# Combining two expert outputs per token: twelve-token tiles in four buffers, and sixteen-token tiles in three with per-token arithmetic

## The chip, the cores and the metric

The kernel runs on one core of a Trainium2 chip. A core has several engines with instruction streams of their own; here VectorE (DVE), ScalarE (ACT) and SyncE (SP) matter. VectorE and ScalarE compute on the core's on-chip memory, which has 128 partitions. Transfers between the chip's large memory (HBM) and the on-chip memory are issued by SyncE or ScalarE and carried out by 16 DMA engines. The metric is the device time of one execution in microseconds (us), the median of several runs. The span, which the profile uses, runs from the first to the last instruction of one profiled execution.

## The reference

```python
batch, seq, hidden, n_experts, k = 16, 1024, 512, 8, 2
# expert_outputs: (batch, seq, k, hidden) float32; combine_weights: (batch, seq, k) float32

def reference(expert_outputs, combine_weights):
    weights = combine_weights[..., np.newaxis]
    return np.sum(expert_outputs * weights, axis=2).astype(np.float32)
```

Each of the 16 x 1024 = 16384 tokens has two vectors of 512 numbers and two weights. The output is the weighted sum of the two vectors. A token is 4 KB of input and 2 KB of output; in all 67 MB are read and 34 MB written. With 128 partitions, each partition handles 128 tokens.

## The kernel before

The tokens of a partition are cut into ten tiles of 12 and a last one of 8. Each tile is loaded, combined in place and stored from the same buffer: the results fill the first half of the tile's bytes. Four buffers rotate, so the load of a tile waits until the store of the tile four places earlier has landed.

The layout: `main` tokens per partition lie in one part of the arrays, and the last tile in a second part, so that each partition reads one contiguous run per tile.

```python
    J, LAST = 12, 8
    main = per - LAST            # per is 128
    eo = expert_outputs.rearrange("b s k h -> (b s) (k h)")
    ...
    def rows(x):
        a = x[0 : P * main, :].rearrange("(p t) f -> p t f", p=P)
        b = x[P * main : n, :].rearrange("(p t) f -> p t f", p=P)
        return lambda t, c: a[:, t : t + c, :] if t < main else b[:, t - main : t - main + c, :]
    ...
    last = main // J
    wpool = ctx.enter_context(tc.tile_pool(name="w", bufs=1))
    ipool = ctx.enter_context(tc.tile_pool(name="in", bufs=4))
    wt = wpool.tile([P, per * k], dt)            # all weights, loaded once through ScalarE's queue
    ...
```

The loop over tiles. Loads go through SyncE's queue. The first load is split in 2 and 10 tokens.

```python
    for g in range(last + 1):
        et = ipool.tile([P, J, k * h], dt)
        ot = et.rearrange("p j f -> p (j f)")[:, 0 : J * h].rearrange("p (j f) -> p j f", f=h)
        t0, c = g * J, J if g < last else LAST

        for a, m in ((0, 2), (2, c - 2)) if g == 0 else ((0, c),):
            nc.sync.dma_start(
                out=et[:, a : a + m],
                in_=eo(t0 + a, m),
                max_dma_last_dim=k * h * 4 if g + a == 0 else None,
            )
```

The first nine tiles are combined by two large VectorE instructions, a product of the whole tile with the weights (line 78) and a sum of its two halves (line 79). Their stores go through ScalarE's queue (line 80).

```python
        if g < last - 1:
            wb = wt[:, g * J * k : (g + 1) * J * k].unsqueeze(2).to_broadcast([P, J * k, h])
            ek = et.rearrange("p j (k h) -> p (j k) h", k=k)
            nc.vector.tensor_tensor(out=ek, in0=ek, in1=wb, op=mult)
            nc.vector.tensor_tensor(out=ot, in0=et[:, :, 0:h], in1=et[:, :, h : 2 * h], op=add)
            nc.scalar.dma_start(out=o(t0, c), in_=ot)
            continue
```

The tenth tile has its first products on ScalarE, a token at a time (line 86), and the second product and the sum as two VectorE instructions (lines 101 and 102). The last tile takes, per token, one ScalarE product and one VectorE multiply-add (line 90). The stores of these two go through SyncE's queue (line 103).

```python
        for i in range(c):
            t = t0 + i
            nc.scalar.activation(
                out=et[:, i, 0:h], in_=et[:, i, 0:h], func=copy, scale=wt[:, 2 * t : 2 * t + 1]
            )
            if g == last:
                nc.vector.scalar_tensor_tensor(
                    out=ot[:, i, :], in0=et[:, i, h : 2 * h],
                    scalar=wt[:, 2 * t + 1 : 2 * t + 2],
                    in1=et[:, i, 0:h], op0=mult, op1=add,
                )
        if g < last:
            ...                                   # w1, x1: second weights, second halves
            nc.vector.tensor_tensor(out=x1, in0=x1, in1=w1.to_broadcast([P, c, h]), op=mult)
            nc.vector.tensor_tensor(out=ot, in0=et[:, :, 0:h], in1=x1, op=add)
        nc.sync.dma_start(out=o(t0, c), in_=ot[:, 0:c])
```

Of the kernel before, what the change touches and what calls it, by code (L numbers as in the profile page):

```python
# [1 line left out]

# [4 lines left out]


@with_exitstack
def kernel(  # L10
    ctx: ExitStack,
    tc: tile.TileContext,
    expert_outputs: bass.AP,
    combine_weights: bass.AP,
    out: bass.AP,
):

    nc = tc.nc  # L20
    b, s, k, h = expert_outputs.shape
    assert k == 2
    n = b * s
    P = nc.NUM_PARTITIONS
    per = n // P
    assert per * P == n
    J, LAST = 12, 8
    main = per - LAST
    assert main % J == 0
    eo = expert_outputs.rearrange("b s k h -> (b s) (k h)")  # L30
    cw = combine_weights.rearrange("b s k -> (b s) k")
    o = out.rearrange("b s h -> (b s) h")
# [7 lines that stand above are left out]
    eo, cw, o = rows(eo), rows(cw), rows(o)  # L40

    dt = mybir.dt.float32
    mult = mybir.AluOpType.mult
    add = mybir.AluOpType.add
    copy = mybir.ActivationFunctionType.Copy

    last = main // J

    wpool = ctx.enter_context(tc.tile_pool(name="w", bufs=1))
    ipool = ctx.enter_context(tc.tile_pool(name="in", bufs=4))  # L50

    wt = wpool.tile([P, per * k], dt)

    for t, c in ((0, main), (main, LAST)):
        nc.scalar.dma_start(
            out=wt[:, k * t : k * (t + c)].rearrange("p (t k) -> p t k", k=k), in_=cw(t, c)
        )

    warm = wpool.tile([P, 1], dt)
    nc.scalar.activation(out=warm, in_=nc.const_aps.tensor(1.0, (P, 1), dt), func=copy)  # L60

    for g in range(last + 1):
        et = ipool.tile([P, J, k * h], dt)

        ot = et.rearrange("p j f -> p (j f)")[:, 0 : J * h].rearrange("p (j f) -> p j f", f=h)
        t0, c = g * J, J if g < last else LAST

        for a, m in ((0, 2), (2, c - 2)) if g == 0 else ((0, c),):
            nc.sync.dma_start(  # L69
                out=et[:, a : a + m],  # L70
                in_=eo(t0 + a, m),
                max_dma_last_dim=k * h * 4 if g + a == 0 else None,
            )
        if g < last - 1:

            wb = wt[:, g * J * k : (g + 1) * J * k].unsqueeze(2).to_broadcast([P, J * k, h])
            ek = et.rearrange("p j (k h) -> p (j k) h", k=k)
            nc.vector.tensor_tensor(out=ek, in0=ek, in1=wb, op=mult)  # L78
            nc.vector.tensor_tensor(out=ot, in0=et[:, :, 0:h], in1=et[:, :, h : 2 * h], op=add)  # L79
            nc.scalar.dma_start(out=o(t0, c), in_=ot)  # L80
            continue


        for i in range(c):
            t = t0 + i
            nc.scalar.activation(  # L86
                out=et[:, i, 0:h], in_=et[:, i, 0:h], func=copy, scale=wt[:, 2 * t : 2 * t + 1]
            )
            if g == last:
                nc.vector.scalar_tensor_tensor(  # L90
                    out=ot[:, i, :],
                    in0=et[:, i, h : 2 * h],
                    scalar=wt[:, 2 * t + 1 : 2 * t + 2],
                    in1=et[:, i, 0:h],
                    op0=mult,
                    op1=add,
                )
        if g < last:
            w1 = wt.rearrange("p (t k) -> p t k", k=k)[:, t0 : t0 + c, 1:2]
            x1 = et[:, :, h : 2 * h]  # L100
            nc.vector.tensor_tensor(out=x1, in0=x1, in1=w1.to_broadcast([P, c, h]), op=mult)  # L101
            nc.vector.tensor_tensor(out=ot, in0=et[:, :, 0:h], in1=x1, op=add)  # L102
        nc.sync.dma_start(out=o(t0, c), in_=ot[:, 0:c])


# [1 line left out]
_INS = ['expert_outputs', 'combine_weights']  # L107
_OUTS = [((16, 1024, 512), 'float32')]


# [23 lines left out]
```

## Time and profile before

| What | Value |
|---|---|
| time, median of 3 runs | 239.17 us (238.93 to 240.34) |
| span of the profiled execution | 237.3 us |
| VectorE busy | 193.9 us |
| ScalarE busy | 14.0 us |
| HBM read and written | 67.24 MB and 33.55 MB, 425 GB/s over the span |
| load of a 12-token tile | 6144 KB, nine times, median 29.9 us from issue to landing |
| store of a 12-token tile | 3072 KB, nine times through ScalarE's queue, median 32.7 us from issue to landing |

Busy time of an engine is the sum of its instructions' durations; two engines can be busy at once. The time from issue to landing of a transfer includes what it spends behind others in its queue. A packet is the piece of a transfer that a DMA engine moves in one go. The chain of waits follows the work that ended last back to the start, at each step to what released it. In a line of instruction groups, L78 means line 78 of the kernel, and `et<-in_expert_outputs_dram` a load into a tile, `out_dram<-et` a store.

### The profile page before, as it was taken

How to read it: one execution, taken by the hardware profiler on the slowest of the kernel's cores; microseconds unless marked ns; L12 is line 12 of the kernel's file. 1: busy time of each engine (PE TensorE's matmuls, PEld its weight loads, DVE VectorE, ACT ScalarE, POOL GpSimd, SP SyncE). 2: the span in 40 equal slices, each digit the busy share in tenths (PEclk: the TensorE clock that was granted, in tenths of full speed). 3: DMA queues.
4: the chain of work that ended last, by engine and by line, in shares of the span. 5: the costliest groups of instructions: out<-in, count | busy, mean ns of one | idle time of the engine just before them, and what ended most of it. 6: DMA issues, size and time to landing. Idle time of an engine off the chain costs nothing.

```text
span 237.3 us, 154 instructions
## 1 busy us (share of the span) xinstructions
DVE 193.9 (82%) x28; ACT 14.0 (6%) x22; POOL 0.2 (0%) x4
## 2 busy tenths in 40 slices
DVE  0008999999999999999999879969996998785710
ACT  2000000000000000000000000000000000740800
POOL 0000000000000000000000000000000000000000
DMA  8999999989899999999897999999997979999997
GB/s 308 443 456 406 398 431 497 398 356 505 356 439 435 427 464 464 398 398 522 348 522 344 452 427 435 464 464 398 398 522 340 530 336 460 458 403 442 402 438 309
DMA packets 3728, 100.80 MB, mean 425 GB/s; under 512 B 528, under 2 KB 656, under 8 KB 912
## 3 DMA queue, kind: packets, MB, share of 16 engines
q1 hardware_dynamic: 2144, 72.35, 71.1%
q10 hardware_dynamic: 1584, 28.44, 27.9%
HBM read 67.24 MB, written 33.55 MB: 425 GB/s over the span
## 4 chain that ended last, share of the span: by engine, by line
DMA 59%; DVE 33%; ACT 2%; DVEq 0%; ACTq 0%; issue 0%; SPq 0%
DMA et<-in_expert_outputs_dram 30%; DMA out_dram<-et 29%; DVE et L78 22%; DVE et L79 11%; ACT et L86 2%; DVE et L90 1%; DVEq L129 0%; ACTq L129 0%; SPq L69 0%; DVEq L78 0%; ACTq L86 0%
## 5 line engine op out<-in xcount | busy, mean ns | idle before, releaser
L78 DVE TENSOR_TENSOR et<-et,wt 128x12288 f32<-128x12288 f32 x9 | 116.6, 12955 | 25.2 <-DMA et<-in_expert_outputs_dram 25.2
L79 DVE TENSOR_TENSOR et<-et 128x6144 f32<-128x6144 f32 x9 | 59.0, 6558 | 0.3
L86 ACT ACTIVATE et<-et,wt 128x512 f32<-128x512 f32 x20 | 12.5, 707 | 209.2 <-DMA et<-in_expert_outputs_dram 209.2
L90 DVE SCALAR_TENSOR_TENSOR et<-et,wt 128x512 f32<-128x512 f32 x8 | 5.6, 748 | 3.9 <-ACT et L86 3.7
L101 DVE TENSOR_TENSOR et<-et,wt 128x6144 f32<-128x6144 f32 x1 | 6.6, 6559 | 2.3 <-DMA et<-in_expert_outputs_dram 2.3
L102 DVE TENSOR_TENSOR et<-et 128x6144 f32<-128x6144 f32 x1 | 6.6, 6559 | 0.9 <-ACT et L86 0.9
L60 ACT ACT_TABLE_LOAD x1 | 1.3, 1283 | 1.7 <-issue 1.7
L60 ACT ACTIVATE warm<-const-float32-1.0 128x1 f32<-128x1 f32 x1 | 0.2, 202 | 0.0
L118 POOL MEMSET const-bfloat16-1.0<- 128x1 bf16 x1 | 0.1, 102 | 0.0
L118 POOL MEMSET const-uint8-127<- 128x1 uint8 x1 | 0.1, 102 | 0.0
L118 POOL MEMSET const-float32-0.0<- 128x1 f32 x1 | 0.1, 99 | 0.2 <-issue 0.2
L118 POOL MEMSET const-float32-1.0<- 128x1 f32 x1 | 0.1, 99 | 0.0
## 6 DMA issues: line engine op xcount, KB each, us to landing
et<-in_expert_outputs_dram SPq DMA_DIRECT2D x9, 6144.0 KB, 29.9
out_dram<-et ACTq DMA_DIRECT2D x9, 3072.0 KB, 32.7
et<-in_expert_outputs_dram SPq DMA_DIRECT2D x1, 5120.0 KB, 17.3
et<-in_expert_outputs_dram SPq DMA_DIRECT2D x1, 4096.0 KB, 25.1
out_dram<-et SPq DMA_DIRECT2D x1, 3072.0 KB, 14.6
out_dram<-et SPq DMA_DIRECT2D x1, 2048.0 KB, 10.0
et<-in_expert_outputs_dram SPq DMA_DIRECT2D x1, 1024.0 KB, 5.4
wt<-in_combine_weights_dram ACTq DMA_DIRECT2D x1, 120.0 KB, 4.4
```

The costliest lines, as they stand in the source:

```text
L60: nc.scalar.activation(out=warm, in_=nc.const_aps.tensor(1.0, (P, 1), dt), func=copy)
L78: nc.vector.tensor_tensor(out=ek, in0=ek, in1=wb, op=mult)
L79: nc.vector.tensor_tensor(out=ot, in0=et[:, :, 0:h], in1=et[:, :, h : 2 * h], op=add)
L86: nc.scalar.activation(out=et[:, i, 0:h], in_=et[:, i, 0:h], func=copy, scale=wt[:, 2 * t : 2 * t + 1])
L90: nc.vector.scalar_tensor_tensor(out=ot[:, i, :], in0=et[:, i, h : 2 * h], scalar=wt[:, 2 * t + 1 : 2 * t + 2], in1=et[:, i, 0:h], op0=mul ...
L101: nc.vector.tensor_tensor(out=x1, in0=x1, in1=w1.to_broadcast([P, c, h]), op=mult)
L102: nc.vector.tensor_tensor(out=ot, in0=et[:, :, 0:h], in1=x1, op=add)
L118: nc = _bacc.Bacc("TRN2", target_bir_lowering=False, num_devices=1)
```

## The change

The tiles become 16 tokens: seven of them, and a last one of the same size, in three buffers in place of four. A row of a load, one partition's part of a tile, is 64 KB, and a row of a store 32 KB. The large VectorE instructions go: in every tile each token takes one ScalarE product and one VectorE multiply-add. The first load is split in 2 and 14 tokens; the last tile is loaded, combined and stored in parts of 12 and 4. The stores go through ScalarE's queue, those of the last tile through SyncE's. It is meant to take work off VectorE, to share it with ScalarE, and to move the same bytes in fewer and longer transfers.

```diff
-    J, LAST = 12, 8
-    main = per - LAST
+    J = 16
+    main = per - J
 ...
-    ipool = ctx.enter_context(tc.tile_pool(name="in", bufs=4))
+    ipool = ctx.enter_context(tc.tile_pool(name="in", bufs=3))
 ...
-    for t, c in ((0, main), (main, LAST)):
+    for t, c in ((0, main), (main, J)):
 ...
-        t0, c = g * J, J if g < last else LAST
+        t0 = g * J
-        for a, m in ((0, 2), (2, c - 2)) if g == 0 else ((0, c),):
+        for a, m in {0: ((0, 2), (2, 14)), last: ((0, 12), (12, 4))}.get(g, ((0, J),)):
             nc.sync.dma_start(
 ...
-        if g < last - 1:
-            ...   # the two large VectorE instructions and their store, as above
-            continue
-        for i in range(c):
-            t = t0 + i
-            nc.scalar.activation(...)
-            if g == last:
+        for a, m in ((0, 12), (12, 4)) if g == last else ((0, J),):
+            for i in range(a, a + m):
+                t = t0 + i
+                nc.scalar.activation(
+                    out=et[:, i, 0:h], in_=et[:, i, 0:h], func=copy, scale=wt[:, 2 * t : 2 * t + 1]
+                )
                 nc.vector.scalar_tensor_tensor(
                     out=ot[:, i, :],
 ...
-        if g < last:
-            ...   # second product and sum of the tenth tile
-        nc.sync.dma_start(out=o(t0, c), in_=ot[:, 0:c])
+            store = nc.scalar if g < last else nc.sync
+            store.dma_start(out=o(t0 + a, m), in_=ot[:, a : a + m])
```

More of the change, by code (lines that the diff above doesn't have):

```diff
@@ L73 @@
             )
-        if g < last - 1:
[L76 to L80, printed above, removed]
-            continue
-        for i in range(c):
-            t = t0 + i
-            nc.scalar.activation(
-                out=et[:, i, 0:h], in_=et[:, i, 0:h], func=copy, scale=wt[:, 2 * t : 2 * t + 1]
-            )
-            if g == last:
+        for a, m in ((0, 12), (12, 4)) if g == last else ((0, J),):
[4 more added lines that the diff above has]
+                )
                 nc.vector.scalar_tensor_tensor(
@@ L97 @@
                 )
-        if g < last:
[L99 to L102, printed above, removed]
-        nc.sync.dma_start(out=o(t0, c), in_=ot[:, 0:c])
+            store = nc.scalar if g < last else nc.sync
+            store.dma_start(out=o(t0 + a, m), in_=ot[:, a : a + m])
 _INS = ['expert_outputs', 'combine_weights']
```

## The prediction

> **What bounds the kernel now.** I read four views, in this order. First the page: the busy shares, the slices and the queues.
>
> ```profile
> DVE 193.9 (82%) x28; ACT 14.0 (6%) x22; POOL 0.2 (0%) x4
> DMA  8999999989899999999897999999997979999997
> DMA packets 3728, 100.80 MB, mean 425 GB/s; under 512 B 528, under 2 KB 656, under 8 KB 912
> q1 hardware_dynamic: 2144, 72.35, 71.1%
> q10 hardware_dynamic: 1584, 28.44, 27.9%
> ```
>
> VectorE is busy 82% of the span, but the two DMA queues (q1 is SyncE's, q10 ScalarE's) together fill 71.1 + 27.9 = 99.0% of the time of the 16 DMA engines. Two limits cannot both hold; the one at 99% does, if it holds in every stage. So second, the chain of waits:
>
> ```profile
> DMA 59%; DVE 33%; ACT 2%; DVEq 0%; ACTq 0%; issue 0%; SPq 0%
> ```
>
> A third of the chain is VectorE. In order of time those are three tiles from 18.6 to 77.1 us and one from 137.7 to 157.2 us: four tiles of 19.5 us, 78 us. To see whether VectorE really holds the kernel there, third, the busy time by stage (length, then DVE, ACT, POOL, clock, DMA share, GB/s):
>
> ```profile
> 18.60:38.00 19.40, 19.33 (x2) 0.00 (x0) 0.00 (x0) 1.00 1.03 446
> 78.00:108.00 30.00, 29.97 (x3) 0.00 (x0) 0.00 (x0) 1.00 1.00 434
> 138.00:168.00 30.00, 27.75 (x3) 0.00 (x0) 0.00 (x0) 1.00 1.01 436
> 220.00:226.50 6.50, 5.57 (x8) 4.94 (x8) 0.00 (x0) 1.00 1.03 442
> 231.50:235.00 3.50, 0.00 (x0) 0.00 (x0) 0.00 (x0) 1.00 1.04 445
> ```
>
> In all of them the DMA engines are full (a share over 1 is a packet counted in the stretch where it starts). The chain takes one releaser at each step, and a tile that computes while older tiles move is on it by name only. Fourth, the timeline of SyncE shows the beat of the loads:
>
> ```profile
> 85.86 0.33 SPq L69 DMA_DIRECT2D et<-in_expert_outputs_dram  x1
> 107.68 0.33 SPq L69 DMA_DIRECT2D et<-in_expert_outputs_dram  x1
> 129.40 0.33 SPq L69 DMA_DIRECT2D et<-in_expert_outputs_dram  x1
> ```
>
> A tile each 21.8 us, where VectorE needs 19.5. The packet records explain 21.8. Each DMA engine carries 8 of the 128 rows of a transfer, one packet a row. Median packet times: 48 KB 1815 ns, 40 KB 1514, 32 KB 1213, 24 KB 912, 16 KB 611; the 4 KB packets of the first load average 201. So a row costs 9 ns + 37.6 ns per KB, whether load or store (16, 24 and 32 KB fall on one line with the rest). Eight load rows and eight store rows are 8 x (1.815 + 0.912) = 21.8 us: the beat of the loads. The kernel moves rows back to back from about 1.8 us to 236 us.
>
> [...] 21.8 us is one load row and one store row in turn, so loads get two thirds of the bytes while both queues have work. [...] the row times here give 1024 B / 37.6 ns = 27.2 GB/s per engine, 435 for 16. [...] The rows stand 480 KB apart before and 448 KB after; no run so far shows 448. [...]
>
> **The change part by part.**
>
> *Arithmetic.* It removes nine pairs of VectorE products and sums (12.95 + 6.56 us for 12 tokens, 1.63 us a token) and the mixed tile before the last. Every token now takes what the last eight took:
>
> ```profile
> L86 ACT ACTIVATE et<-et,wt x20: 704/706/722, 203.0 to 224.2; 128x512 f32<-128x512 f32 x20
> L90 DVE SCALAR_TENSOR_TENSOR et<-et,wt x8: 746/746/753, 220.7 to 225.7; 128x512 f32<-128x512 f32 x8
> ```
>
> The eight ScalarE products took 5.01 us in all, 0.63 a token; the eight multiply-adds 5.78 us, 0.72 a token, the first of them 0.84 us after the load landed (219.85 to 220.69). The two overlap, so a 16-token tile takes 0.84 + 16 x 0.72 = 12.4 us from landing to store, against 19.5 for 12 tokens. VectorE falls to 128 x 0.75 = 95 us busy, ScalarE rises to 128 x 0.71 + 1.5 = 92 us. Neither is near the span. On the end they are worth nothing as long as the queues stay full.
>
> *Transfers.* The bytes are the same. I add up one DMA engine's rows, times 8.
> Before: first load 2 x 0.201 + 1.514; nine loads of 48 KB 16.335; last load 1.213; ten stores of 24 KB 9.120; last store 0.611; weights 0.055. Sum 29.25, times 8 = 234.0 us.
> After: 2 x 0.201 + 2.116 (56 KB); six loads of 64 KB, by the line 9 + 64 x 37.6 = 2417 ns (an estimate, as are 56 KB and 8 KB), 14.50; 1.815 + 0.611; seven stores of 32 KB 8.49; 0.912 + 0.310; weights 0.055. Sum 29.21, times 8 = 233.7 us.
> The difference is the 9 ns of some rows saved: 0.3 us.
>
> *Buffers.* 3 x 16 = 48 tokens, as 4 x 12 was. Does a queue run dry? The first rows move about 1 us after issue (none before 1.6 us), and I allow 1 us from last row to landing. The second part of load 0 lands near 23.5; its 14 tokens are done at 23.5 + 0.84 + 14 x 0.72 = 34.4. Store 0 then shares with load 1 and load 2, 2.417 + 1.213 = 3.63 us a pair, 29.0 us for eight pairs, so it lands near 64.6 and releases load 3. Load 2, with less of its rows moved, lands near 74.3: SyncE's queue still has some 9 us of work when load 3 comes in. Tile 2 is done at 74.3 + 12.4 = 86.7, and store 1 lands near 93.7: ScalarE's queue still has some 5 us after issue time. From there each beat repeats at 29.0 us, with the same margins. ScalarE now issues the stores behind its own arithmetic and waits there for VectorE; it has 29 us for 12.4 of work, so that wait costs nothing.
>
> *End.* Load 7 is released by store 4, near 181. Its 12-token part lands near 214.7, computed at 214.7 + 0.84 + 12 x 0.72 = 224.2. The 4-token part leaves SyncE's queue near 226, store 6 leaves ScalarE's near 224. So the 12-token store, with a microsecond of issue, comes in at 225.3, just in time. It and the 4-token store then take 8 x (0.912 + 0.310) = 9.8 us: near 236, landed near 237. Before, the end was as tight: last store 10.0 us from issue to landing. I count 0 here, with a risk of 0.5 to 1 us.
>
> Sum: 237.3 - 0.3 = 237.0 us of span; the time stands 1.9 above the span (239.17 against 237.3): 238.9 us.
>
> **The rivals.**
>
> *VectorE was the bound.* For it: 82% busy and 78 us of the chain. If those 78 us of tiles (48 tokens at 1.63) shrank to 0.72 a token, 43 us would go, and the time would be 196 us. Against it: rows need 233.7 us at a rate that no size exceeds. Even without any start or end the gain could be at most 237.3 - 233.7 = 3.6 us, 1.5%. I give this nearly nothing.
>
> *Three large buffers starve a queue.* Each new load waits for a whole 4 MB store, and the unit is a third larger. If the margins of 9 and 5 us were misjudged, 1 to 3 us per beat would be lost in four or five beats: 243 to 252 us. Against it: the ratio of bytes and the 48 tokens are unchanged, the queues are served row by row, and compute is 7 us shorter per tile.
>
> *The 64 KB row.* It lies beyond the sizes measured (48 KB at most). If it moved as two packets, loads and stores would share evenly; stores would land sooner and loads later, with full queues all the same; the steps above with even turns end 0.4 us later: 239.3 us. If long rows or the 448 KB distance cost 5% of the load rate, 8 x 19.4 x 0.05 = 7.8 us would come on top: 246.6 us. The straight line from 16 to 48 KB speaks against it.
>
> *The end comes apart.* If the 12-token store misses its moment, the engines idle for what it is late: at 0.8 us a token 1 us, so 239.9 us.
>
> **Range and chances.** The middle is 238.9. A quieter end or fewer long rows (48 KB rows averaged 1823 ns, not 1815, some 0.6 us over the kernel) take it to 237.7; a late last store and the scatter of the times before (238.93 to 240.34) take it to 240.6. Faster by over 2% means under 234.4, a span of 232.5, less than the rows need: 0.02. Slower by over 2%, above 244.0, needs starved queues or slow rows: 0.06. Within 2%: 0.92.
>
> **What would show it.** Right: the queues' shares again sum to about 99%, packets of 64 KB take about 2417 ns, loads are issued 29.0 us apart, VectorE is busy near 95 us with waits on loads, and the slices of the DMA show no hole but the first. Wrong: load issues more than 30 us apart or a lower DMA share in the middle (starved buffers); packets of 64 KB above 2.5 us (the row); a gap in the DMA between 222 and 228 us (the end); or a span under 234 us, which would break the rule that rows cost what their bytes cost.

## The result, and the profile after

| | time, median | span of the profiled execution |
|---|---|---|
| before | 239.52 us (238.93 to 240.34) | 237.3 us |
| changed | 241.18 us (240.93 to 241.78) | 239.8 us |

The ratio of changed to before is 1.0082, with a 95% interval of 1.0061 to 1.0103. The change makes the kernel 0.8% slower. The prediction had 238.9 us and a range up to 240.6. Executions of the kernel before fall in two groups, 73 of 107 near 239.0 us and 34 near 240.3, at the same clock and for a reason that no run here shows; the ratios average over both, while the trace and the span of before are of the first.

The changed kernel's page, busy shares, slices and queues:

```profile
DVE 87.0 (36%) x128; ACT 81.0 (34%) x130; POOL 0.2 (0%) x4
DMA  9999999999999999999999999999999999999895
DMA packets 3155, 100.82 MB, mean 420 GB/s; under 512 B 464, under 2 KB 592, under 8 KB 848
q1 hardware_dynamic: 1856, 71.30, 69.4%
q10 hardware_dynamic: 1296, 29.49, 28.7%
q14 instruction: 3, 0.02, 0.0%
```

VectorE's work has more than halved, as meant, and the DMA engines are full in every slice up to the last three. What is new is the last line: a third queue, named instruction, with three packets. The page of the kernel before has no such line. Those packets are 8 KB each and take 0.309 us; together they are 0.02 of 100.82 MB. (In both traces such packets also lie before the span begins.)

The chain of waits and the beat of the loads in the changed kernel:

```profile
DMA 85%; DVE 6%; ACT 4%; issue 1%; SPq 1%; DVEq 0%; ACTq 0%
```

```profile
67.29 0.33 SPq L68 DMA_DIRECT2D et<-in_expert_outputs_dram  x1
96.25 0.33 SPq L68 DMA_DIRECT2D et<-in_expert_outputs_dram  x1
125.78 0.33 SPq L68 DMA_DIRECT2D et<-in_expert_outputs_dram  x1
154.79 0.33 SPq L68 DMA_DIRECT2D et<-in_expert_outputs_dram  x1
```

The loads are 28.96, 29.53 and 29.01 us apart. Rows cost what they should: 64 KB packets have a median of 2418 ns. So the middle runs at the rate of the rows, and the loss is at the end. Busy time by stage there (length, DVE, ACT, POOL, clock, DMA share, GB/s), changed kernel:

```profile
226.00:228.00 2.00, 0.49 (x1) 0.00 (x0) 0.00 (x0) 1.00 0.62 254
236.00:237.00 1.00, 0.00 (x0) 0.00 (x0) 0.00 (x0) 1.00 1.04 434
237.00:238.00 1.00, 0.00 (x0) 0.00 (x0) 0.00 (x0) 1.00 0.12 49
238.00:239.00 1.00, 0.00 (x0) 0.00 (x0) 0.00 (x0) 1.00 0.02 8
```

The same stretches of the kernel before:

```profile
226.00:228.00 2.00, 0.46 (x1) 0.00 (x0) 0.00 (x0) 1.00 0.92 393
236.00:237.00 1.00, 0.00 (x0) 0.00 (x0) 0.00 (x0) 1.00 0.00 0
```

Two things differ. Between 226 and 228 us the DMA engines are idle for a while (0.62). And after 237.4 us a little traffic goes on: one DMA engine of sixteen is a share of 0.06. The packet records do not name their engine, but a packet starts where another ends (in both traces every packet over 2 KB from 30 to 215 us does, within 5 ns), so they can be strung into sixteen chains, one for each engine; this is a reconstruction, and where several packets end within a few ns, the rows that an engine still has to carry (8 of each transfer) settle the join. Fifteen chains of the changed kernel end by 237.4 us, the last at 238.4; in the kernel before all end by 236.2. The late chain carried two of the three instruction packets, at 84.2 and 226.5 us; the third, at 111.5, lies on another. The row that starts where such a packet ends was longer too: a 64 KB row at 84.5 us took 2952 ns in place of 2418, one at 111.8 us 2661, a 16 KB row at 226.8 us 1255 in place of 611. So a packet put its engine back by 0.55 to 0.95 us (0.31 plus the longer row), in queues that leave no pause in which to make it up.

This gave two theories. **Fetch:** the packets of the instruction queue come with the many small instructions (411 in the span in place of 154) and move on the same DMA engines; an engine that carries one falls behind for good, and each landing waits for the latest engine. (No view shows what these packets hold: that they fetch instructions is the author's reading of the queue's name.) **End:** faster tiles start their stores earlier, stores take turns from loads (from 112 to 134 us of the kernel before, each queue moved 144 packets), the last load lands later, and too little store work is left to cover the last tile's arithmetic. The tile sizes and buffers themselves are a third suspect, **shape**.

### The profile page after: what moved, and what is told of

Its sections match the earlier page's. It is cut to its first block, busy times and chain, and to the rows that moved or that the text cites. A ratio compares the mean times of both kernels' runs of the same rounds, so it can differ in the third digit from the quotient of the medians.

```text
span 239.8 us, 411 instructions
## 1 busy us (share of the span) xinstructions
DVE 87.0 (36%) x128; ACT 81.0 (34%) x130; POOL 0.2 (0%) x4
## 2 busy tenths in 40 slices
DMA packets 3155, 100.82 MB, mean 420 GB/s; under 512 B 464, under 2 KB 592, under 8 KB 848
## 4 chain that ended last, share of the span: by engine, by line
DMA 85%; DVE 6%; ACT 4%; issue 1%; SPq 1%; DVEq 0%; ACTq 0%
DMA et<-in_expert_outputs_dram 54%; DMA out_dram<-et 31%; DVE et L79 6%; ACT et L76 4%; SPq L68 1%; DVEq L114 0%; ACTq L76 0%
## 5 line engine op out<-in xcount | busy, mean ns | idle before, releaser
L79 DVE SCALAR_TENSOR_TENSOR et<-et,wt 128x512 f32<-128x512 f32 x128 | 87.0, 746 | 145.6 <-ACT et L76 144.0
L76 ACT ACTIVATE et<-et,wt 128x512 f32<-128x512 f32 x128 | 79.5, 708 | 149.0 <-DMA et<-in_expert_outputs_dram 149.0
```

What stands on the lines that cost most here:

```text
L76: nc.scalar.activation(out=et[:, i, 0:h], in_=et[:, i, 0:h], func=copy, scale=wt[:, 2 * t : 2 * t + 1])
L79: nc.vector.scalar_tensor_tensor(out=ot[:, i, :], in0=et[:, i, h : 2 * h], scalar=wt[:, 2 * t + 1 : 2 * t + 2], in1=et[:, i, 0:h], op0=mul ...
```

## The experiments

Each is compared with the kernel before by the ratio of times; spans and packets are from one profiled execution. Packets means 8 KB packets of the instruction queue within the span. A memset is an instruction that fills a tile with a constant; here it fills one number per partition, on the otherwise idle GpSimd (POOL).

| Run | what | instructions | packets | ratio to before (95%) | span, us |
|---|---|---|---|---|---|
| changed | | 411 | 3 | 1.0082 (1.0061 to 1.0103) | 239.8 |
| e1 | arithmetic of the change in the old tiles | 421 | 3 | 1.0082 (1.0058 to 1.0107) | 239.9 |
| e15 | before + 384 idle memsets | 539 | 3 | 1.0062 (1.0045 to 1.0080) | 238.9 |
| e2 | before + 640 idle memsets | 795 | 5 | 1.0107 (1.0080 to 1.0135) | 240.5 |
| e8 | before + 1280 idle memsets | 1435 | 10 | 1.0270 (1.0240 to 1.0300) | 243.4 |
| e12 | changed + 640 idle memsets | 1052 | 8 | 1.0128 (1.0105 to 1.0151) | 241.4 |
| e3 | changed, fewer instructions | 212 | 1 | 1.0102 (1.0076 to 1.0128) | 241.1 |
| e13 | changed, ScalarE products, order held | 261 | 1 | 1.0193 (1.0171 to 1.0215) | 242.3 |
| e14 | e13 + 384 idle memsets | 646 | 4 | 1.0216 (1.0198 to 1.0235) | 242.7 |
| e9 | before, ScalarE products | 269 | 1 | 1.0534 (1.0499 to 1.0568) | 251.0 |
| e11 | e9 with VectorE's order held | 269 | 1 | 1.0015 (0.9995 to 1.0034) | 237.5 |
| e16 | e11 + 256 idle memsets | 526 | 3 | 1.0140 (1.0105 to 1.0174) | 241.0 |
| e10 | before, few instructions, early stores | 219 | 2 | 1.0005 (0.9991 to 1.0019) | 237.8 |
| e5 | tile sizes and buffers alone | 143 | 0 | 1.0408 (1.0363 to 1.0452) | 246.7 |
| e4 | changed, end in 11 + 5 | 412 | 3 | 1.0093 (1.0064 to 1.0122) | 240.4 |
| e6 | changed, first store 4 us later | 413 | 3 | 1.0102 (1.0075 to 1.0129) | 239.4 |
| e7 | before, first load in one piece | 154 | 0 | 1.0019 (1.0004 to 1.0033) | 237.1 |

### The arithmetic alone

```diff
-        if g < last - 1:
-            ...   # two large VectorE instructions, store, continue
         for i in range(c):
             nc.scalar.activation(...)
-            if g == last:
-                nc.vector.scalar_tensor_tensor(...)
-        if g < last:
-            ...   # large product and sum of the tenth tile
+            nc.vector.scalar_tensor_tensor(...)
```

> The kernel before with its tiles of 12 and 8 in four buffers, and only the arithmetic of the change: one ScalarE product and one VectorE multiply-add for every token. Fetch theory (the longer instruction streams, some 390 against 154 instructions, are fetched by DMA during the run, 8 KB at a time on one DMA engine, and that engine falls behind by 0.5 to 0.9 us each time, and every landing waits for it): about three instruction packets appear inside the span, the span is 1 to 2 us over the 237.3 of before. Rival, the tile sizes (64 KB rows, three buffers, end in 12 + 4): the time stays within 0.4 us of before.

Measured: 1.0082, the same as the whole change, with three instruction packets, at 84.5, 106.2 and 221.3 us. The new tile sizes, the three buffers and the 12 + 4 end are not needed for the loss; the per-token arithmetic brings as much by itself. Both theories leave a mark here. The DMA share falls between 230 and 234 us, because the last load lands at 226.29 us, where it landed at 219.85 before:

```profile
230.00:232.00 2.00, 2.00 (x4) 1.30 (x3) 0.00 (x0) 1.00 0.46 197
232.00:234.00 2.00, 0.82 (x2) 0.00 (x0) 0.00 (x0) 1.00 0.34 143
```

Part of that delay is the wait for one engine: fourteen chains end the rows of the last load by 224.0 us, the one with the packet of 106.2 us at 224.4, and the one with the packets of 84.5 and 221.3 us at 225.7.

### Instruction packets and nothing else

```diff
+    idle = wpool.tile([P, 1], dt)
+    for _ in range(640):
+        nc.gpsimd.memset(idle, 0.0)
     for g in range(last + 1):
```

> The kernel before, to which 640 tiny memsets on the idle GpSimd are added, whose tile nobody reads. Fetch theory: 640 instructions[...] are about five packets of 8 KB on the instruction queue during the first part of the run; the DMA engine or engines that carry them end late, the span grows by 0.5 us at least, up to 4 us if one engine carries all. Rival theories (tile sizes, arithmetic, end): no change, within 0.3 us, because neither a load, a store nor an instruction of VectorE or ScalarE is touched.

Measured: 1.0107, a span of 240.5 us, five packets, about 20 us apart from 11.4 to 91.6 us. No load, store, ScalarE or VectorE instruction is changed. The instruction queue (packets, MB, share) and the end of this run by stage, same columns:

```profile
q14 instruction: 5, 0.04, 0.0%
```

```profile
234.00:236.00 2.00, 0.00 (x0) 0.00 (x0) 0.00 (x0) 1.00 0.96 410
236.00:237.00 1.00, 0.00 (x0) 0.00 (x0) 0.00 (x0) 1.00 0.08 33
237.00:238.00 1.00, 0.00 (x0) 0.00 (x0) 0.00 (x0) 1.00 0.04 16
238.00:239.00 1.00, 0.00 (x0) 0.00 (x0) 0.00 (x0) 1.00 0.08 33
```

Fifteen engines end by 236.5 us, 0.3 later than without the memsets; one goes on alone, at about a sixteenth of the rate, to 239.3 us. In the reconstruction all five packets lie on this one chain, so that their delays add up. It is already 2.3 us behind the others when the third tile's load ends (51.5 against 49.3 us) and 3.3 behind (139.6 against 136.4 for most) in the middle of the run: a lag made in the first 92 us is still there at the end. This is the fetch theory seen by itself. If the busy GpSimd slowed all transfers alike, all sixteen engines would be late; fifteen of them are only 0.3 us later.

> The kernel before with 1280 idle memsets on GpSimd, twice as many as in the run with 640. Fetch theory: ten instruction packets of 8 KB in place of five, each putting its DMA engine back by 0.5 to 0.9 us for good; the span grows by 5 to 7 us over 237.3, in place of 3.2 with five. If the 3.2 us came from something else that GpSimd does (its busy time[...]), packets and span need not go together; if the late engine can catch up, the span stays near 240.5.

With `range(1280)`: ten packets, ratio 1.0270, a span of 243.4 us, 6.1 us over before where five packets cost 3.2. Twice the packets cost about twice the time, as expected. All ten lie on one chain again, which ends at 242.1 us, the others by 239.3:

```profile
q14 instruction: 10, 0.08, 0.1%
```

That is one packet for each 128 memsets: five for 640, ten for 1280, none without them.

The changed kernel has three packets. With `range(384)` the kernel before has three as well:

> The kernel before with 384 idle memsets on GpSimd: three packets, as many as the changed kernel has, and nothing else changed. If three packets are enough for the loss of the changed kernel, 1.004 to 1.010 of before (between the runs with one or two packets, not measurable, and that with five, 1.0107). If the number of packets is not what costs the changed kernel, within 0.3%.

Measured: 1.0062 (1.0045 to 1.0080), three packets, by 52.4 us all done, and this end:

```profile
234.00:236.00 2.00, 0.00 (x0) 0.00 (x0) 0.00 (x0) 1.00 0.92 393
237.00:238.00 1.00, 0.00 (x0) 0.00 (x0) 0.00 (x0) 1.00 0.04 16
```

Again the engine with all three packets ends last, at 237.6 us; one other ends at 237.1, the rest by 236.3. Three packets and nothing else bring about three quarters of the changed kernel's 0.8%. That the numbers come so close is in part chance: here all three fall on one engine and there is no pause at the end, in the changed kernel two do and there is one.

> The changed kernel with the 640 idle memsets on GpSimd. Fetch theory: eight packets in place of three; five packets cost the kernel before 3.2 us, so about 3 us over the changed kernel, 244.2, or 1 us less where the gap at the end lets late engines catch up (243 to 244.5). If the packets were not what costs the changed kernel, because the end has room for a late engine, it stays within 1 us of 241.2.

The same 640 memsets in the changed kernel: eight packets, 1.0128, a span of 241.4 us, so 1.6 us over the changed kernel and less than expected (3). Its end shows where the rest went:

```profile
226.00:228.00 2.00, 2.00 (x4) 1.31 (x3) 0.00 (x0) 1.00 0.34 143
228.00:229.00 1.00, 1.00 (x2) 0.00 (x0) 0.00 (x0) 1.00 0.04 16
229.00:230.00 1.00, 0.03 (x1) 0.00 (x0) 0.00 (x0) 1.00 0.77 328
```

Fifteen engines stop between 226.5 and 227.5 us and stand still until 229.9, waiting for the store of the last tile's first 12 tokens (VectorE is still busy with them, for the late engine ended its rows of that load at 218.1 us, the others by 214.2); the late engine works through its rest in that time, and all sixteen then end together, at 239.7 to 240.0 us. A late engine thus costs in one of two ways: alone at the end, or as a late landing that makes the others wait.

### Fewer instructions

```diff
-        for a, m in ((0, 12), (12, 4)) if g == last else ((0, J),):
+        if g < last:
+            for i in range(8):
+                nc.scalar.activation(...)                  # first products of 8 tokens
+            nc.vector.tensor_tensor(out=x0, ...)           # first products of the other 8
+            nc.vector.tensor_tensor(out=x1, ...)           # second products of all 16
+            nc.vector.tensor_tensor(out=ot, ..., op=add)
+            st = nc.scalar.dma_start(out=o(t0, J), in_=ot)
+            continue
+        for a, m in ((0, 12), (12, 4)):
```

> The changed kernel with its tiles of 16, three buffers and end of 12 + 4, but with few instructions in the first seven tiles: ScalarE takes only eight first products, VectorE does the rest in three large instructions. Fetch theory: no instruction packets in the span; the last of the 16 DMA engines ends with the others; the span falls from 239.8 to about 238.3 (the gap at the end, about 0.5 to 1 us, stays). Rival, the rows and buffers: the span stays at 239.5 to 240. If a longer combination (22 us in place of 12.4) mattered, it would be slower than the changed kernel.

Measured: 1.0102, span 241.1 us, one packet, at 169.3 us. The expected fall did not come, and the run settles nothing on fetch, because it changes a second thing: a tile now takes 22 us. The first store is issued at 45.2 us in place of 33.6, and the store queue runs dry between tiles (from 121.7 to 131.3 us, for one). Where stores begin again beside running loads, rows are longer for a moment: 53 of the 64 KB packets took over 100 ns more than their median, up to 4288 ns, and over the run that is 1.8 us per engine where the changed kernel has 1.0.

The same idea in the old tiles of 12, where the beat leaves more room:

```diff
-        if g < last - 1: ...                               # two large VectorE instructions
+        for i in range(12):                                # e9; 6 in e10
+            nc.scalar.activation(...)
+        # e10 only: first products of the other 6 tokens on VectorE
+        nc.vector.tensor_tensor(out=x1, ..., op=mult)
+        nc.vector.tensor_tensor(out=ot, ..., op=add)
```

> The kernel before, tiles of 12 in four buffers, with the first ten tiles combined as its tenth tile is: twelve ScalarE products, then one large VectorE product and one large sum. ScalarE has as many instructions as in the changed kernel (130), VectorE only 28. A tile takes about 14 us in place of 19.5, so stores start earlier than before. Fetch theory: the packets that belong to VectorE's stream vanish, one packet or two of ScalarE's stay; the time is 0.5 to 1.3 us over before, in place of 2.5 us in the run with the arithmetic alone. End theory alone (early stores): as slow as the run with the arithmetic alone, 241 to 241.7, or at least 1.5 us over before.

Measured: 1.0534, far outside both theories, and for a reason of its own. VectorE's program had come out in another order, with the product of a following tile ahead of the sum of the tile before it in several places; those sums, and with them their stores, waited for loads that came later. ScalarE, whose next products stand behind those stores, waits for the sums (us in total, times, longest):

```profile
ACT et L79 <- DVE et L98: 101.7, 6, 37.3
```

So it was run again with that order held:

```diff
+            with tc.issue_after(sm.ins) if g else ExitStack():
                 nc.vector.tensor_tensor(out=x1, ..., op=mult)
+            sm = nc.vector.tensor_tensor(out=ot, ..., op=add)
```

> The run with ScalarE products in tiles of 12, with VectorE's order held (the product of a tile after the sum of the tile before it), so that no sum waits for the next load. ScalarE 130 instructions, VectorE 28, a tile in 14 us. Fetch theory: one packet in the span as in that run; 0.5 to 0.9 us over before, 239.6 to 240.0. End theory alone: stores 5 us earlier than before bring the same gap at the end as the arithmetic alone, 241 to 241.7.

Measured: 1.0015 with an interval that reaches below 1, one packet, span 237.5 us, 0.2 over before. ScalarE has its 130 small instructions, a tile takes 14 us in place of 19.5 and the last load lands at 223.75 us, 4 us later than before, and yet no gap opens:

```profile
226.00:228.00 2.00, 1.90 (x4) 2.00 (x4) 0.00 (x0) 1.00 0.94 406
234.00:236.00 2.00, 0.00 (x0) 0.00 (x0) 0.00 (x0) 1.00 0.92 393
236.00:237.00 1.00, 0.00 (x0) 0.00 (x0) 0.00 (x0) 1.00 0.01 0
```

To this kernel, which has early stores and no measurable loss, packets were then added, with 256 idle memsets:

> The kernel with ScalarE products in order and tiles of 12 (one packet, 1.0015) with 256 idle memsets on GpSimd: three packets in place of one, in a kernel with early stores. If packets bring the loss: 1.005 to 1.010. If early stores with packets open the gap at the end as well: up to 1.012. If neither: 1.000 to 1.003.

Measured: 1.0140 (1.0105 to 1.0174), more than was expected and more than three packets cost the kernel before. Here a gap does open:

```profile
230.00:232.00 2.00, 2.00 (x4) 2.00 (x4) 0.00 (x0) 1.00 0.92 393
232.00:234.00 2.00, 1.69 (x3) 0.17 (x1) 0.00 (x0) 1.00 0.12 49
234.00:236.00 2.00, 0.00 (x0) 0.00 (x0) 0.00 (x0) 1.00 0.95 397
```

The last load lands at 227.16 us in place of 223.75: two engines end its rows at 225.2 and 225.8 us, the others by 222.6. For most of 232 to 234 us the DMA engines have nothing to move while VectorE ends its last tokens. Tiles, stores and buffers are those of e11; only packets were added. So fetch and end are not two rivals but one chain: packets make an engine late, the late engine makes the last load late, and early stores leave too little behind it to cover that. Neither early stores with a single packet (e11) nor three packets alone (e15: 0.6%) cost as much as both.

> The kernel before, tiles of 12 in four buffers, with six ScalarE products per tile and three large VectorE instructions: about 76 ScalarE and 37 VectorE instructions, and a tile in about 16.5 us in place of 19.5. Fetch theory: no instruction packet in the span, or one; the time is that of before, 239.1, within 0.7 us. End theory alone: the stores are earlier than before by 3 us, the last load lands later, and the time is 0.5 to 1.5 us over before without any packet.

Measured: 1.0005 (0.9991 to 1.0019), two packets (at 166.8 and 231.7 us), span 237.8 us, a tile in 16.5 us, no gap. With one or two packets, stores 3 to 5 us earlier cost nothing that the ratio shows, and 0.2 to 0.5 us of span. That also bounds the packets: one or two do not cost 0.6 us each, as ten do on average. In e10 the two packets lie on two chains, which end last, at 236.4 and 236.6 us, the others by 236.1; in e11 the chain with the packet ends at 236.35, the others by 236.2. On different engines the delays do not add up; in the runs with memsets they do.

### The shape alone, and the changed shape with fewer instructions

```diff
-        for a, m in ((0, 12), (12, 4)) if g == last else ((0, J),):
+        if g < last:
+            ...   # the two large VectorE instructions of the kernel before, and the store
+            continue
+        for a, m in ((0, 12), (12, 4)):
```

> The changed kernel's tiles of 16, three buffers and end of 12 + 4, with the two large VectorE instructions of the kernel before in the first seven tiles (tile sizes alone). A tile then takes 26 us of VectorE against a beat of 29 us of the DMA engines. If the shape costs nothing by itself and only the short combination made it possible: stores come 14 us later, the store queue runs dry between tiles, and the loads behind it wait for a store; the span grows to 241 to 244. If three buffers with late stores still keep the queues full: 237 to 238.5, and no instruction packets.

Measured: 1.0408, worse than either theory said. There are no packets. The large instructions take 26 us for 16 tokens, so stores come too late for three buffers:

```profile
DMA  9998999989996997998997999979998999999985
```

The 64 KB packets are longer by 4.0 us per engine over the run and the store rows by 1.7, most of it where transfers go on after a pause, and idle time is another 3.8 us. So the three buffers of 16 do need the short combination; with it (e1 against the changed kernel, the same ratio) they cost nothing that these runs show.

Two more runs tried to take packets out of the changed shape and put them back. The edit is that of e3 with sixteen ScalarE products, one large product and one large sum per tile, in order, and for the second run 384 idle memsets.

> The changed kernel's tiles of 16, three buffers and 12 + 4 end, with sixteen ScalarE products and two large VectorE instructions for a tile, in order (17.5 us in place of 12.4; 22 in the earlier try). ScalarE 130 instructions, VectorE about 30. Fetch theory: one packet; the time comes back to 0 to 0.8 us over before, 239.1 to 239.9. If the shape with its end is what costs the changed kernel: 241 to 241.5 as before. If 17.5 us is too slow for three buffers, pauses of the DMA engines in the middle and 240 to 243 without packets, which would leave the question open.

> The same kernel with 384 idle memsets on GpSimd: four packets in place of one, everything else the same, store times too. Fetch theory: 1 to 2.5 us over that kernel, by engines that end late. Otherwise: within 0.4 us of it.

Measured: 1.0193 and 1.0216. The third outcome named came true: 17.5 us for a tile is already too long for three buffers. Stores resume after pauses, 78 of the 64 KB packets are more than 100 ns too long (2.7 us per engine over the run), unevenly, so that one engine ends at 241.0 us, two at 240.5 and the others by 238.9, with a single packet. Three packets more then add little (0.2%, with intervals that overlap). Three engines are late here although there is one packet, so others than packets make engines late; whether that hides the three packets more is not shown. In this shape the packets could not be taken away by themselves.

### The end

```diff
-    (0, 12), (12, 4)
+    (0, 11), (11, 5)     # loads, arithmetic and stores of the last tile
```

> The changed kernel with the last tile in parts of 11 and 5 tokens in place of 12 and 4, so that the first store of the end is ready about 1.7 us earlier. End theory alone (the DMA engines idle about 1 us between 226.4 and 227.4 us because the 12-token store comes late): the gap closes and the span falls by 1.0 us, to 238.8. With the fetch theory as well: the gap had let the late DMA engine catch up; 15 engines end 1 us earlier, the late one does not, and the span falls by only 0.2 to 0.4 us.

Measured: 1.0093, span 240.4 us: no gain. The first gap closed (the 11-token store is issued at 225.23 us) and another opened before the 5-token store, issued at 233.9: its tokens landed only at 229.68 us, because a packet at 226.0 us sat on one engine in the middle of that load: this engine ended its rows at 229.2 us, the others by 227.4.

```diff
+            if g == 0:
+                for _ in range(2):                       # after the products of tile 0
+                    nc.scalar.activation(out=hold, in_=..., func=copy)   # 128x3072, read by nobody
             store.dma_start(...)
```

> The changed kernel, with the first store held back by about 4 us on ScalarE (two idle copies of 128x3072 between the first tile's products and its store). End theory: earlier stores take turns from the loads, so the last load lands later and too little store work is left to cover the last tile's arithmetic; with the first store 4 us later, the last 12-token load lands about 1.3 us earlier, the gap near 226.4 to 227.4 us closes, and the span falls by 0.3 to 1.0 us. Fetch theory alone: the three instruction packets stay, the late engine sets the end, and the span stays within 0.3 us of the 239.8 of the changed kernel.

Measured: 1.0102, span 239.4 us. The end theory's mechanism holds, its size does not. With the first store 4 us later the last 12-token load lands at 216.53 in place of 217.31 us, and the queues stay full:

```profile
226.00:228.00 2.00, 0.00 (x0) 0.00 (x0) 0.00 (x0) 1.00 0.94 389
234.00:236.00 2.00, 0.00 (x0) 0.00 (x0) 0.00 (x0) 1.00 0.98 410
236.00:237.00 1.00, 0.00 (x0) 0.00 (x0) 0.00 (x0) 1.00 0.43 180
237.00:238.00 1.00, 0.00 (x0) 0.00 (x0) 0.00 (x0) 1.00 0.16 66
```

Thirteen engines now end by 236.6 us, close to the kernel before, and three between 237.8 and 238.0 (a share of 0.16): the span is only 0.4 us less, and the time is not better. With the gap gone the loss stays, and it is that of late engines. But they are not all late by packets. In the reconstruction one of the three carried two packets (at 85.9 and 226.2 us); the other two carried none, and are late by rows that took longer where the first stores joined the loads (1.9 and 2.2 us in all, where most engines have about 0.7).

### A piece less at the start

```diff
-        for a, m in ((0, 2), (2, c - 2)) if g == 0 else ((0, c),):
+        for a, m in ((0, c),):
 ...
-                max_dma_last_dim=k * h * 4 if g + a == 0 else None,
```

> The kernel before, with its first tile loaded by one transfer of 48 KB rows in place of sixteen 4 KB rows and eight 40 KB rows per DMA engine. By the row times: 8 x 1.815 = 14.5 us in place of 3.2 + 12.1 = 15.3 us, so 0.8 us less if the start of the first packets costs the same; VectorE waits for the whole tile in both. Expected 238.4 against 239.2. If the start-up delay of the first packets is hidden in the 4 KB rows (some took 1028 ns in place of 158), the gain is only 0.2 to 0.4 us.

Measured: 1.0019 (1.0004 to 1.0033), no gain. The first 48 KB rows are longer: those between 1.7 and 4.6 us took up to 2882 ns in place of 1815. In the kernel before it was 4 KB rows that came first, and they took up to 1028 ns in place of 159. No version here beats the kernel before; by the ratio e10 and e11 equal it.

## Why the prediction was wrong, by its own steps

**What bounds the kernel** was right: the DMA engines, by row time. The shares of the two data queues still sum to 98.1%, and the rival "VectorE was the bound" is dead, since VectorE fell from 193.9 to 87.0 us busy for no gain.

**Transfers** was right in every term that it had: 2418 ns for a 64 KB row (2417 predicted), 1213 for a 32 KB row, a beat of 29.0 us. The rivals of slow long rows, of split rows and of the 448 KB distance (their 5% was an assumption of the author's) fall with it. One small term was missing: where the first store meets running loads, the load rows are longer, and over the run that makes 1.0 us per engine for the 64 KB rows against 0.6 for the 48 KB rows before.

**Buffers** was right: in the middle no queue ran dry, and by e1 shape and buffers cost nothing measurable beside this arithmetic. That they would cost 4% with slower arithmetic was not foreseen.

**Arithmetic** is the step that failed. It priced 256 small instructions by their engine time (a little high: 95 and 92 us, measured 87.0 and 81.0), found that neither engine was near the span, and wrote that they are worth nothing on the end "as long as the queues stay full". But with the small instructions came packets of the instruction queue, three of 0.309 us each, on the DMA engines, which bound the kernel. The sum had no term for that. Three packets of 8 KB, 0.02% of the bytes, are enough (1.0062 in e15), because they do not spread over sixteen engines: each made one engine 0.55 to 0.95 us late in the changed kernel, several on one engine add up, and the end is that of the latest. That such packets lengthen the run by themselves is shown by the idle memsets (1.6, 3.2 and 6.1 us of span for three, five and ten). That they turn early stores into a loss is shown by e16 against e11. That this is what costs the changed kernel its time is read from its trace (the latest engine, 1.0 us behind the fifteen others, is the one with two packets) and from e1 (as many packets, the same loss, old shape, and the last load held up by the engines with packets). e6 fits only in part: the gap closed and late engines left, two of the three without packets. The direct proof, the changed kernel with its tile time but without its packets, stays open: e3 and e13 took packets away and made the tile too slow for three buffers.

**End** counted 0 with a risk of 0.5 to 1 us, and the trace has the gap between 222 and 228 us that the prediction named as a sign of being wrong: fifteen engines stop between 226.3 and 227.0 us and go on at 227.4 to 227.5, 0.8 us on the mean. The 12-token store, "just in time" at 225.3 in the prediction, was issued at 226.5, because its load landed at 217.31 us in place of 214.7. Of these 2.6 us, 0.7 is the wait for the late engine, which ended its rows of that load at 215.6 us, the others by 214.9. Another 0.7 is a landing that took 1.7 us from the last row's end, where the prediction allowed 1; the rest is rows that came 1.2 us later than the prediction had them, about 1.0 of it the longer load rows. So packets are not the only cause of the gap, and what it would be without them was not measured.

The terms, on the last row's end: 236.2 before, minus 0.3 for rows, plus 0.4 for longer load rows at the first store, plus 0.8 for the gap makes 237.1 (measured 237.4 for fifteen engines, so 0.3 stays unexplained), and 1.0 for the late engine brings it to 238.4. The range was too narrow above, since it knew no cost that grows with the number of instructions (1.6, 3.2 and 6.1 us for 384, 640 and 1280 memsets).

## What to carry to other kernels

Where DMA engines have no pause, count instructions as well as their time: here a change that traded few large instructions for many small ones (154 to 411) came with three instruction packets on those engines, and one late engine set the landing of transfers that are spread over all (its rows of the last 12-token load ended at 215.6 us, the others' by 214.9). Look for the instruction queue in the profile, and at the last few microseconds for a DMA share of one sixteenth or less (0.04 to 0.08 in e2). Engine time off the critical path was free here, and saving it bought nothing (VectorE from 193.9 to 87.0 us busy, 0.8% slower); tile size and tile time had to be changed together, because three buffers of 16 did not hold with stores as late as the large instructions made them (26 us for a tile, 1.0408 in e5).

## What was not expected of the hardware

- Instruction packets of 8 KB appeared during the run, one for each further 128 memsets (three for 384, five for 640, ten for 1280). In the changed kernel each took 0.309 us, and the data row after it 0.24 to 0.64 us longer. In the reconstruction all packets of e2, of e8 and of e15 fall on one DMA engine.
- A lag of one DMA engine was hardly made up while its queues were full: 3.3 us behind at 140 us, 2.8 at the end (e2).
- Load rows were up to 1.06 us longer (3474 against 2418 ns, between 34 and 39 us of the changed kernel) where the first store joined running loads, and again where stores resumed after a pause (up to 4288 ns in e3).
- Stores landed later where loads ran beside them: a store's last row ended 2.15 us before its landing beside 48 KB loads (before, near 193 us), 2.7 to 2.8 us beside 64 KB loads (changed, near 64 and 181 us), and 0.33 us with no load running (before, last store). The differences, 1.8 and 2.4 us, are close to one load row (1815 and 2418 ns).
